# A hybrid decoder step: the output projection by seven half-size products a pair, and the residual added later and by columns

## The chip, the cores and the metric

The kernel runs on one core of one Trainium2 chip. The core has a matrix engine (TensorE, PE in the profile), a vector engine (VectorE, DVE), a scalar engine (ScalarE, ACT), GpSimd (POOL) and a sync engine (SP) that only issues transfers; transfers run on 16 DMA engines. ACT, DVE and PE each take their instructions in program order and wait at the head of their queue; POOL computes a little and issues its own transfers, among them all that add to what lies at their destination. The metric is the device time of one execution in microseconds (us), the median of several.

## The reference, and what is computed

One step of a decoder layer for 1024 prompt tokens and 8 x 8 sample tokens, T = 1088 token columns, width 1024, all in fp32:

```
xn = RMSNorm(x)
q, k, v, a, b, gate_a, gate_b = split(xn @ w_in)
A = windowed attention(q, k, v) @ w_o ;  B = silu(LayerNorm(conv31(a * sigmoid(b)))) @ w_pb
h = x + (sigmoid(gate_a) * A + sigmoid(gate_b) * B) @ w_out        # the output projection
up = RMSNorm(h) @ w_up                                             # 1024 -> 2 x 2816
y = RMSNorm(h + (silu(conv3(up)[:2816]) * conv3(up)[2816:]) @ w_down)
```

Call the merged branches (the bracket ahead of w_out) M. What the change touches is M @ w_out, the RMSNorm and the first up-projections that follow, and the place where h, the residual, is added to the result of w_down.

## The kernel before

Activations lie with the features in the 128 partitions and the tokens along the row. A product in fp32 is made as three matmuls of rounded words (`mm3`): every operand x is held as a high word, x rounded, and a low word, x minus the high word; the matmuls are high by high, high by low and low by high. Making the words is a *split* (`split_ps`, for weights `w_parts`): ACT casts, DVE subtracts.

The stages, with their place in the profiled execution (us): the input projection with attention and convolution in between, ending in the two gates (to some 648); w_o (to 748); w_pb, with M formed and split as it comes out (`do_pb`, to 843); the output projection (843 to 942); three plain up-projections f = 0, 1, 2 (to 1015); nineteen further ones as *pairs* (1015 to 1464); the down-projection in three *rounds* (to 1626), and a tail that does the last four features plainly and applies the last norm (to the end).

A *pair* is a Strassen-Winograd product: a 2 x 2 product of halves takes seven half-size products in place of eight, at the price of sums of weights (s1 to s4), sums of activations (T1 to T4) and additions of results. In the up stage the sums of activations are made once (`sums`, all four quarters of the tokens), the sums of weights on DVE for each pair (`plan_pair`, line 1172). In the down stage the sums of weights are made ahead in DRAM by POOL's transfers (`folds`, line 617, tensor d_wd), six dependent stages a pair, two transfers in the first two stages and one in the others.

The output projection is plain: eight blocks m of 128 output features, each over four quarters of 272 tokens and eight blocks of inputs, 8 x 4 x 8 x 3 = 768 matmuls of 272 columns. Evacuation (`ev_out`) adds x from DRAM, squares on ACT and sums the squares on DVE for the norm. The last four m run quarter by quarter, and after each quarter `norm2` makes the norm, splits the normed quarter, and has POOL store h to DRAM (d_h, line 1006). `sums` follows in f = 0; it forms each normed value again from its two words (line 1131). A plain up-projection ends in `finish`, a convolution on ACT and DVE (line 1082), gate, and a store of the product (d_x) from which the down stage reads its operands (x, line 1304); in a pair, `finish` of the feature is placed in the queues 100 steps later (UP_LATER).

In the last round, (r, j) = (2, 0) in the code, POOL adds h from d_h onto the results held in H by sixteen accumulating transfers of 272 KB, four after each of the products n = 0, 1, 3 and 4 (line 1421). The tail then walks through the columns in three chunks of 352, 352 and 256 (TAIL_CHUNKS).

The order on each engine is made by a scheduler from the priorities of the program; `later` moves a piece back, and `in_order` ties a piece to the instructions written just ahead of it. The functions are these:

## Time and profile before

| | us |
|---|---|
| median of three runs (lowest, highest) | 1683.46 (1680.57, 1689.4) |
| the profiled execution | 1688.82 |
| its span | 1686.9 |
| PE busy in it | 1658.0 (98%) |
| DVE busy | 1320.3 (78%) |
| ACT busy | 885.2 (52%) |
| POOL busy | 299.9 (18%) |

The span is the time from the first to the last instruction in the trace; 1.9 us of the profiled execution lie outside it. "Busy" is the time in which an engine had at least one instruction in work, and waits are put down to the engine or transfer that ended them. The row of PE's clock gives the share of full speed that was granted. A matmul's row lasts longer than the distance to the next one, since matmuls are pipelined.

### The profile page before, as it was taken

How to read it: one execution, taken by the hardware profiler on the slowest of the kernel's cores; microseconds unless marked ns; L12 is line 12 of the kernel's file. 1: busy time of each engine (PE TensorE's matmuls, PEld its weight loads, DVE VectorE, ACT ScalarE, POOL GpSimd, SP SyncE). 2: the span in 40 equal slices, each digit the busy share in tenths (PEclk: the TensorE clock that was granted, in tenths of full speed). 3: DMA queues.
4: the chain of work that ended last, by engine and by line, in shares of the span. 5: the costliest groups of instructions: out<-in, count | busy, mean ns of one | idle time of the engine just before them, and what ended most of it. 6: DMA issues, size and time to landing. Idle time of an engine off the chain costs nothing. (4 is left out here: it accounts for less than half of the span.)

```text
span 1686.9 us, 30229 instructions
## 1 busy us (share of the span) xinstructions
PE 1658.0 (98%) x11656; PEld 1639.0 (97%) x11656; DVE 1320.3 (78%) x2400; ACT 885.2 (52%) x1807; POOL 299.9 (18%) x541
## 2 busy tenths in 40 slices
PE   9999999999999999999999998999999999999998
PEld 8999999999999999999999997999999999998998
DVE  7899999999669995865546896778778777976556
ACT  7434477743588745973333454444444446833222
POOL 0210112130011111110000154333333210001100
PEclk9999999999999999999999999999999999999999
DMA  6122213242211255544343336676766544758713
GB/s 210 42 51 70 63 58 115 61 143 58 82 45 47 81 211 170 174 161 135 126 141 105 89 126 166 179 180 173 180 173 173 142 109 174 259 181 234 173 65 106
DMA packets 114015, 220.56 MB, mean 131 GB/s; under 512 B 24384, under 2 KB 63440, under 8 KB 113568
## 3 DMA queue, kind: packets, MB, share of 16 engines
q1 hardware_dynamic: 85328, 136.99, 26.5%
q0 software_dynamic: 27968, 81.12, 18.2%
q8 instruction: 91, 1.49, 0.4%
q10 hardware_dynamic: 576, 0.53, 0.1%
q14 instruction: 52, 0.43, 0.1%
HBM read 158.21 MB, written 81.24 MB: 142 GB/s over the span
## 5 line engine op out<-in xcount | busy, mean ns | idle before, releaser
L198 PE MATMUL mm<-xh,whi 128*128 128x384 f32 (+1 forms) x920 | 306.9, 334 | 0.8 <-ACT whi L179 0.8
L199 PE MATMUL mm<-xl,whi 128*128 128x384 f32 (+1 forms) x920 | 301.2, 327 | 0.0
L200 PE MATMUL mm<-xh,wlo 128*128 128x384 f32 (+1 forms) x920 | 300.9, 327 | 0.0
L198 PEld LDWEIGHTS mm<-xh,whi 128*128 128x128 f32 x920 | 173.5, 189 | 2.2 <-ACT whi L179 1.4
L199 PEld LDWEIGHTS mm<-xl,whi 128*128 128x128 f32 x920 | 173.6, 189 | 1.1 <-DVE xl L262 0.2
L200 PEld LDWEIGHTS mm<-xh,wlo 128*128 128x128 f32 x920 | 173.2, 188 | 0.1
L1082 DVE SCALAR_TENSOR_TENSOR acc<-st,fc,acc 128x1104 f32<-128x1104 f32 x88 | 119.7, 1364 | 3.2 <-ACT acc L1080 1.4
L198 PE MATMUL mm<-mh,whi 128*128 128x272 f32 x368 | 106.7, 290 | 1.0 <-ACT st L1073 1.0
L199 PE MATMUL mm<-ml,whi 128*128 128x272 f32 x368 | 106.1, 288 | 0.0
L200 PE MATMUL mm<-mh,wlo 128*128 128x272 f32 x360 | 104.1, 289 | 0.0
L179 ACT CAST whi<-wraw 128x1024 fp32r<-128x1024 f32 (+1 forms) x71 | 69.1, 977 | 64.2 <-PE mm L199 49.1
L180 DVE TENSOR_TENSOR wlo<-wraw,whi 128x1024 fp32r<-128x1024 f32 (+1 forms) x71 | 80.0, 1130 | 16.8 <-ACT whi L179 16.6
L477 DVE SCALAR_TENSOR_TENSOR bt<-u,consts,bt 128x513 f32<-128x513 f32 x120 | 89.6, 747 | 0.6
L477 DVE SCALAR_TENSOR_TENSOR c<-sm,hsum,c 128x512 f32<-128x512 f32 x120 | 89.4, 745 | 0.6
L477 DVE SCALAR_TENSOR_TENSOR c<-u,consts,c 128x512 f32<-128x512 f32 x112 | 83.4, 744 | 0.2
L198 PE MATMUL mm<-th,whi 128*128 128x272 f32 x240 | 70.0, 292 | 4.5 <-DVE st L1204 3.6
L198 PEld LDWEIGHTS mm<-mh,whi 128*128 128x128 f32 x368 | 69.2, 188 | 1.3 <-ACT st L1073 1.3
L199 PE MATMUL mm<-tl,whi 128*128 128x272 f32 x240 | 70.1, 292 | 0.0
L200 PE MATMUL mm<-th,whi 128*128 128x272 f32 x240 | 69.9, 291 | 0.0
L199 PEld LDWEIGHTS mm<-ml,whi 128*128 128x128 f32 x368 | 69.4, 188 | 0.0
L330 ACT ACTIVATE p<-p,nm 128x257 f32<-128x257 f32 (+1 forms) x128 | 62.2, 489 | 12.0 <-DVE nm L325 11.7
L200 PEld LDWEIGHTS mm<-mh,wlo 128*128 128x128 f32 x360 | 67.7, 188 | 0.0
(609 smaller groups left out, 5640.5 us busy)
## 6 DMA issues: line engine op xcount, KB each, us to landing
wraw<-wall SPq DMA_DIRECT2D x113, 512.0 KB, 3.8
d_x<-st POOLq DMA_DIRECT2D x27, 544.0 KB, 6.2
d_wd<-wall POOLq DMA_DIRECT2D x54, 256.0 KB, 5.9
x<-d_x SPq DMA_DIRECT2D x14, 544.0 KB, 5.6
d_x<-acc POOLq DMA_DIRECT2D x9, 816.0 KB, 8.0
wraw<-wall SPq DMA_DIRECT2D x27, 256.0 KB, 4.0
x<-d_x SPq DMA_DIRECT2D x14, 408.0 KB, 3.8
d_wd<-d_wd POOLq DMA_DIRECT2D x18, 256.0 KB, 4.5
```

What stands on the lines that cost most here:

```text
L179: self.nc.scalar.copy(h[:, z], r[:, z])
L180: self.nc.vector.tensor_tensor(l[:, z], r[:, z], h[:, z].bitcast(F32), ALU.subtract)
L198: mm(ps, wh, xh, start=first, stop=False, skip_group_check=more)
L199: mm(ps, wh, xl, start=False, stop=False, skip_group_check=more)
L200: mm(ps, wl, xh, start=False, stop=last, skip_group_check=more)
L330: nc.scalar.activation(pt[:, j, lo:width + 1], pt[:, j, lo:width + 1], AF.Exp, bias=nm[:, j:j + 1], scale=-1.0, accum_out=den[:, j:j + 1])
L477: mac = lambda o, x, w: nc.vector.scalar_tensor_tensor(o, x, w, o, ALU.mult, ALU.add)
L1082: nc.vector.scalar_tensor_tensor(acc, st[:, k:k + AW], fw(f, k), acc, ALU.mult, ALU.add)
```

## The change

**The output projection** takes the blocks m two by two, four pairs of seven half-size products, each over two quarters and four blocks of inputs: 4 x 7 x 2 x 12 = 672 matmuls. The sums of the weights are made in DRAM (d_wo) by POOL, eight transfers of 256 KB a pair in six stages (`fold_stages`), one stage put ahead of each stream of the input phase from the twelfth weight on. T1 is formed and split in `do_pb`, whose blocks now run in the order 0, 4, 1, 5, 2, 6, 3, 7; T2 to T4 are formed there and split in the first pair. The last pair runs by quarters. Results are added up in H, now eight tiles (a quarter by half the features).

**norm2** works in place in H and comes in the order of quarters 2, 0, 3, 1; h is stored by POOL ahead of it. **f = 0 and f = 1** run side by side, quarter by quarter (`plain_side`), norm2 of the next quarter in between; `sums` takes the normed values from H, in two calls, without forming them from words. `finish` of f = 0, 1, 2 is not moved back. Several buffers lie elsewhere.

**The residual** is added by columns: columns 0 to 271, four rows after product 4 and four after product 5 of the last half round (2, 1); columns 272 to 703 after the rounds; columns 704 to 1087 in the first chunk of the tail. Ahead of each group POOL copies one column of the last result ("mark"). The tail's chunks are 272, 432 and 256. `in_order` now covers POOL too.

```diff
-TAIL_CHUNKS = [(0, 352), (352, 352), (704, 256)]
+TAIL_CHUNKS = [(0, 272), (272, 432), (704, 256)]
...
+FOLD_FROM = 12
+PB_ORDER = (0, 4, 1, 5, 2, 6, 3, 7)
+LATE_QUARTERS = (2, 0, 3, 1)
...
+    def fold_stages(self, a, b, c, d, to):
+        s = [to[k] for k in range(4)]
+        return [[(s[0], c), (s[3], a)], [(s[0], d, ALU.add), (s[3], c, ALU.add)], [(s[1], s[0])],
+                [(s[1], a, ALU.add)], [(s[2], s[1])], [(s[2], b, ALU.add)]]
...
+            if FOLD_FROM <= n:
+                with self.in_order():
+                    self.fold(next(out_folds, ()))
...
+                if y == 0 and c == 2:
+                    live["12"], live["t1"] = right, left
+                    add(left, right, left)
+                    for j, (h, l) in enumerate(B[T1]):
+                        self.split_ps(h[:, kk, :], l[:, kk, :], left[:, j * QW:(j + 1) * QW])
+                if y and c == 1:
+                    add(word[T2][:, kk, :], right, live["t1"])
+                    add(word[T3][:, kk, :], live["12"], right)
+                if y and c == 0:
+                    add(word[T4][:, kk, :], left, word[T2][:, kk, :])
...
+        seq = (("A", "11", 0, 0, True), ("E", T1, 1, 1, True), ("A", T2, 0, 1, False), ("E", "22", 0, 1, False),
+               ("A", T3, 1, 1, False), ("C", "21", 0, 0, True), ("A", T4, 1, 0, False))
...
+        def product(p, n, j):
+            bank, b, u, half, fresh = seq[n]
+            m, c = 2 * p + u, 2 * half + j
...
+            hs = H[c, m // 4][:, m % 4, :]
...
+            for k in range(KT // 2):
+                ks = slice(k * P, (k + 1) * P)
+                self.mm3(ps, wh[:, ks], wl[:, ks], xh[:, k, :], xl[:, k, :], fresh and k == 0, k == KT // 2 - 1, not fresh)
...
+            add(hs, t if first else hs, ps, ALU.subtract if u == 0 and bank != "C" else ALU.add)
+            if last:
+                nc.scalar.activation(t if m else ssq[c], hs, AF.Square)
+                if m:
+                    add(ssq[c], ssq[c], t, ALU.add)
...
+                for x in (k, k + 1):
+                    hs = H[c, y][:, x % 4, :]
+                    nc.vector.scalar_tensor_tensor(hs, hs, self.c("g2", x), ssq[c], ALU.mult, ALU.mult)
+                self.split_ps(hh[c][y][:, ks, :], hl[c][y][:, ks, :], H[c, y][:, ks, :])
...
+            for n, c in enumerate(LATE_QUARTERS):
+                norm = norm2(LATE_QUARTERS[n + 1]) if n < 3 else iter(())
+                next(norm, None)
+                if n == 0:
+                    ws += [self.weight(("up", x), 0) for x in fs[2:]]
+                if n == 2:
+                    sums(0)
+                for x in (0, 1, 2, 3) if n < 3 else (2, 3, 0, 1):
+                    self.stream(None, xs, both[x][3], chunks=(c,), w=ws[x], table=QUARTERS)
+                    for _ in norm:
+                        pass
+            sums(1)
+            for f in range(2):
+                finish(f, both[2 * f:2 * f + 2])
...
-                        add(r, hh[c][y][:, ks].bitcast(F32), hl[c][y][:, ks].bitcast(F32))
...
-            if (r, j) == (2, 0):
-                for top, half in {0: ((0, 0),), 1: ((4, 0),), 3: ((0, 1),), 4: ((4, 1),)}.get(n, ()):
-                    cs = slice(half * HT, (half + 1) * HT)
-                    for row in range(top, top + 4):
-                        nc.gpsimd.dma_start(H[row][:, cs], self.d_h[row, :, cs], accum_op=ALU.add)
+            if (r, j) == (2, 1) and n in (4, 5):
+                residual(hs, range(4 * n - 16, 4 * n - 12), slice(*TAIL_CHUNKS[0]))
...
+        residual(hs, range(KT), slice(o1, o1 + w1))
...
+                if c == 0 and m == 4:
+                    residual(hs, range(KT), slice(o1 + w1, T))
```

What this does to the order on the engines, at three places. First **POOL in the input phase**. In the names, p and sp are the tiles of the softmax, into which POOL copies the sink; kp is a load of old keys, d_c and o_cb* are stores, u gets zeros. A bracket names what an instruction waits for; DMASW and DMAHW are landings of transfers. Before:

```order
L319 COPY p_2946<-nsink_83 128x4 [waits PE_49,Activation_49,Pool_49]
L500 DMA d_c_59<-u_1494 128x1024 [waits DMASW4_49,DVE_49]
L672 DMA o_cbp<-u_2383 128x30 [waits DMASW5_49,DVE_49]
L673 DMA o_cbs<-u_2383 1024x1x30 [waits DMAHW5_49,DMASW6_49,DVE_49]
L643 MEMSET u_3032 128x30 [waits DMASW4_49,DMASW3_49]
L644 MEMSET u_3032 128x2
L319 COPY p_2996<-nsink_83 128x4 [waits PE_49,Activation_49,Pool_49]
L411 DMA kp_3322<-kpT 128x256 [waits DMASW7_49,DMASW0_49,PE_49]
```

and now, in the same place:

```order
L320 COPY p_2957<-nsink_84 128x4 [waits PE_49,Activation_49,Pool_49]
L501 DMA d_c_59<-u_1495 128x1024 [waits DMASW6_49,DVE_49]
L611 DMA d_wo_65<-wall 128x512 [waits DMASW7_49,DMASW4_49]
L611 DMA d_wo_65<-wall 128x512 [waits DMASW5_49,DMASW0_49]
L686 DMA o_cbp<-u_2391 128x30 [waits DMASW1_49,DVE_49]
L687 DMA o_cbs<-u_2391 1024x1x30 [waits DMAHW5_49,DMASW2_49,DVE_49]
L611 DMA d_wo_65<-d_wo_65 16x4096 [waits DMASW7_49,DMASW3_49]
L320 COPY p_3007<-nsink_84 128x4 [waits PE_49,Activation_49,Pool_49]
L657 MEMSET u_3045 128x30 [waits DMASW6_49]
L658 MEMSET u_3045 128x2
L412 DMA kp_3336<-kpT 128x256 [waits PE_49]
L611 DMA d_wo_65<-wall 128x512 [waits DMASW3_49]
```

Between the two copies into p three transfers of the sums have come in (two more stand just ahead of the first copy): the second stage, two 128x512 that each wait for a landing of the first, and the third, the 16x4096 one, which waits for a landing of the second. The fourth follows the load of kp and waits for the third.

Second **DVE in f = 0**: the sums for the pairs. Before, each first forms four values from the words mh and ml:

```order
L1131 TENSOR_TENSOR s_10326<-mh_1203_9533,ml_1205_9535 128x544
L1131 TENSOR_TENSOR s_10328<-mh_1245_9855,ml_1247_9857 128x544
L1131 TENSOR_TENSOR s_10330<-mh_1246_9856,ml_1248_9858 128x544
L1131 TENSOR_TENSOR s_10332<-mh_1204_9534,ml_1206_9536 128x544
L1131 TENSOR_TENSOR s_10326<-s_10328,s_10326 128x544 [waits DVE_49]
L1131 TENSOR_TENSOR s_10328<-s_10330,s_10328 128x544 [waits DVE_49]
L228 TENSOR_TENSOR tl_1288_10075<-s_10326,th_1280_10067 128x544 [waits Activation_49]
L1131 TENSOR_TENSOR s_10330<-s_10330,s_10326 128x544 [waits DVE_49]
L228 TENSOR_TENSOR tl_1292_10079<-s_10328,th_1284_10071 128x544 [waits Activation_49]
L1131 TENSOR_TENSOR s_10332<-s_10332,s_10330 128x544 [waits DVE_49]
L228 TENSOR_TENSOR tl_1290_10077<-s_10330,th_1282_10069 128x544 [waits Activation_49]
L1131 TENSOR_TENSOR s_10346<-mh_1203_9533,ml_1205_9535 128x544
```

and now, with th the tiles of H:

```order
L1268 TENSOR_TENSOR th_1136_8921<-th_1140_8925,th_1136_8921 128x544
L229 TENSOR_TENSOR ml_1327_10415<-th_1137_8922,mh_1325_10413 128x544 [waits Activation_49]
L1268 TENSOR_TENSOR th_1140_8925<-th_1141_8926,th_1140_8925 128x544 [waits DVE_49]
L1268 TENSOR_TENSOR th_1136_8921<-th_1140_8925,th_1136_8921 128x544
L1268 TENSOR_TENSOR th_1141_8926<-th_1141_8926,th_1136_8921 128x544 [waits DVE_49]
L1268 TENSOR_TENSOR th_1140_8925<-th_1141_8926,th_1140_8925 128x544 [waits DVE_49]
L1268 TENSOR_TENSOR th_1137_8922<-th_1137_8922,th_1141_8926 128x544 [waits DVE_49]
```

The additions of mh and ml are gone; the four subtractions of each step remain, and the splits follow them.

Third **POOL at the end of the down stage**, the transfers that add h onto the results, whose tiles now bear the names mh to tl. Before, in the first half of the last round, the first eight of sixteen:

```order
L1421 DMA th_1833_15851<-d_h_63 128x544 [waits DMASW2_49,DVE_49]
L1421 DMA th_1835_15860<-d_h_63 128x544 [waits DVE_49]
L1421 DMA tl_1837_15871<-d_h_63 128x544 [waits DVE_49]
L1421 DMA tl_1839_15880<-d_h_63 128x544 [waits DVE_49]
L1421 DMA mh_1822_15802<-d_h_63 128x544 [waits DMAHW6_49,DMASW6_49,DVE_49]
L1421 DMA mh_1824_15811<-d_h_63 128x544 [waits DVE_49]
L1421 DMA ml_1826_15828<-d_h_63 128x544 [waits DMASW0_49,DVE_49]
L1421 DMA ml_1828_15837<-d_h_63 128x544 [waits DMASW1_49,DVE_49]
```

and now, in the second half of it:

```order
L1514 COPY mark_17849<-tl_1804_15880 128x1 [waits DVE_49,Activation_49]
L1517 DMA mh_1787_15802<-d_h_63 128x272 [waits DMASW6_49,PE_49]
L1517 DMA mh_1789_15811<-d_h_63 128x272 [waits PE_49]
L1517 DMA ml_1791_15828<-d_h_63 128x272
L1517 DMA ml_1793_15837<-d_h_63 128x272
L1514 COPY mark_17917<-ml_1793_15837 128x1 [waits DVE_49]
L1517 DMA th_1798_15851<-d_h_63 128x272 [waits DMASW2_49,PE_49]
L1517 DMA th_1800_15860<-d_h_63 128x272 [waits PE_49]
L1517 DMA tl_1802_15871<-d_h_63 128x272 [waits DMASW4_49]
L1517 DMA tl_1804_15880<-d_h_63 128x272 [waits DMASW5_49]
L1514 COPY mark_17975<-tl_1804_15880 128x1 [waits DVE_49,Pool_49]
```

The first eight have half the columns they had, stand in the second half of the round, behind a mark, and two more groups of eight (432 and 384 columns) follow the third mark and a fourth.

More of the change, by code (lines that the diff above doesn't have):

```diff
@@ L1008, in phase_z @@
[L1008 to L1016 removed]
+        z_es.close()
+        l_es, h_es, wt_es = ExitStack(), ExitStack(), ExitStack()
@@ new lines, in phase_z @@
+        pairs = KT // 2
+        for p in range(1, pairs - 1):
+            for n in range(7):
+                i = 7 * p + n
+                w_load2(15 if i < 12 else i + 4 if i < 18 else 28)
+                w_split2(i + 3)
+                for j in range(2):
+                    product(p, n, j)
+        w_split2(28)
+        norm = norm2(2)
+        for j in range(2):
+            for n in range(7):
+                product(pairs - 1, n, j)
+                if n in (4, 6):
+                    store(6 - n + j)
+                if j == 0 and n == 0:
+                    while len(self.w_raw) < n_up + 2:
+                        self.w_load()
+                if j == 0 and n == 4:
+                    with self.in_order():
+                        while len(self.w_hl) < n_up + 2:
+                            self.w_split()
+                if j and n % 2 == 0:
+                    with self.in_order():
+                        next(norm)
+            if not j:
+                next(norm)
@@ L1227, in ffn @@
             plan_pair(f)
-        for f in range(PLAIN):
+        plain_side()
+        for f in range(2, PLAIN):
             plain(f)
-            if f == 0:
-                with self.later(SUM_LATER):
-                    sums()
         steps = [(r, j, n) for r in range(len(ROUNDS)) for j in range(2) for n in range(7)]
@@ L1257, in ffn @@
         free += [(0, f"w{z}{x}") for z in ("hi", "lo") for x in range(2)]
-        free += [(12, f"d{x}") for x in range(3)]
+        free += [(4 * (x < 2), f"th{x}1") for x in range(4)]
         free.sort(key=lambda x: x[0])
@@ L1373, in ffn, with residual @@
         ops = (ALU.add, ALU.subtract, ALU.add, ALU.add, ALU.subtract, ALU.subtract, ALU.subtract)
+        def residual(after, rows, cs):
+            mark = nc.gpsimd.tensor_copy(self.t(dt, [P, 1], "mark", bufs=2), after[:, 0:1])
+            with tc.issue_after(mark.ins):
+                for row in rows:
+                    nc.gpsimd.dma_start(H[row][:, cs], self.d_h[row, :, cs], accum_op=ALU.add)
         for s, (r, j, n) in enumerate(steps):
```

289 lines of the change are left out of this document (170 added, 119 removed).

## The prediction

> **What bounds the kernel now.** First the page: is one engine the limit?
>
> ```profile
> span 1686.9 us, 30229 instructions
> PE 1658.0 (98%) x11656; PEld 1639.0 (97%) x11656; DVE 1320.3 (78%) x2400; ACT 885.2 (52%) x1807; POOL 299.9 (18%) x541
> DVE  7899999999669995865546896778778777976556
> ```
>
> PE is busy for 98% of the span, so two things shorten it: fewer matmuls, and fewer gaps. Next, busy time by stage (columns: length, then busy us and instructions of PE, weight load, DVE, ACT, POOL; the granted clock; DMA share; GB/s).
>
> ```profile
> 843.00:943.00 100.00, 99.88 (x783) 99.01 (x782) 59.35 (x122) 34.03 (x69) 2.70 (x3) 1.00 0.42 125
> 1015.00:1047.00 32.00, 24.25 (x174) 22.97 (x173) 19.86 (x31) 11.88 (x24) 14.01 (x24) 0.95 0.72 195
> 1464.00:1533.00 69.00, 68.69 (x549) 68.47 (x548) 56.90 (x108) 32.16 (x50) 0.00 (x0) 1.00 0.66 204
> 1533.00:1582.00 49.00, 43.97 (x328) 42.69 (x327) 21.57 (x39) 11.60 (x11) 13.95 (x16) 0.97 0.89 207
> ```
>
> The output projection (first row) has no gap: 99.88 us for 783 matmuls, 0.1276 us each. Two stages do: the first pair, idle for 32 - 24.25 = 7.75 us, and the first half of the last round, idle for 49 - 43.97 = 5.03. These idle times are low by some 0.16 us a gap, because a matmul's row lasts 290 ns, not 128 (row in the third part): with five and six gaps, 8.6 and 6.0 us. Who ends the gaps, in each of the two (waiting line, releaser: us, times, longest):
>
> ```profile
> PE mm L198 <- DVE st L1204: 3.6, 1, 3.6
> PE aux L198 <- ACT st L1222: 1.5, 1, 1.5
> PE mm L198 <- ACT st L1073: 1.0, 1, 1.0
> ...
> PE mm L198 <- ACT x L1311: 1.7, 1, 1.7
> PE mm L199 <- DVE x L228: 0.9, 1, 0.9
> ```
>
> In the pair it is ACT's and DVE's evacuation (st); in the round the splits of x, and behind these the chain of waits shows transfers (start, us, what):
>
> ```profile
> 1025.75 0.51 POOL d_x L1110
> 1035.23 8.06 DMA wraw<-wall
> ...
> 1539.95 15.78 DMA x<-d_x
> 1555.83 1.11 ACT x L227
> 1556.97 1.30 DVE x L228
> 1564.50 10.95 DMA x<-d_x
> ```
>
> So the loads of x take 15.78 and 10.95 us. Over the program they take 5.6, and in that window software transfers (POOL's) hold half of the moved time, because POOL adds h there:
>
> ```profile
> x<-d_x SPq DMA_DIRECT2D x14, 544.0 KB, 5.6
> ...
> q0 software_dynamic: 2129, 4.14, 50.3%
> th<-d_h POOLq DMA_DIRECT2D x4, 272.0 KB, 8.5
> ```
>
> A gap may also cost clock. Two stretches after a gap:
>
> ```profile
> 1044.40:1047.80 3.40, 3.33 (x16) 3.33 (x17) 3.17 (x4) 0.21 (x1) 2.58 (x6) 0.56 0.31 127
> 1549.10:1552.50 3.40, 3.40 (x15) 3.40 (x16) 1.27 (x4) 1.04 (x1) 0.86 (x1) 0.51 1.07 271
> ```
>
> After the 3.6 us wait the clock was 0.56 for 3.4 us, and at 1549, behind waits of 1.7 and 0.9, it was 0.51. So the two stages lose another 1.5 and 1.7 us: 10.1 us in the first pair and 7.7 in the round.
>
> The Trainium skill, "TensorE: Matmul & The Clock Gate", section "Why this matters for your kernels", asks for no idle gaps of more than about 3 us to keep the clock. By that, the round's gaps would cost no clock; the row at 1549 shows that two shorter ones did, so here I follow the row. By the page the round's term would be 6.0 instead of 7.7.
>
> **The change part by part.** The durations that I use (line, engine, tiles, shapes, count | busy, mean ns):
>
> ```profile
> L198 PE MATMUL mm<-mh,whi 128*128 128x272 f32 x128 | 37.1, 290 | 0.0
> ...
> L984 DVE TENSOR_TENSOR H<-mm,xr 128x272 f32<-128x272 f32 x32 | 13.6, 434 | 24.5 <-PE mm L200 24.4
> L989 DVE TENSOR_TENSOR ssq<-ssq,xr 128x272 f32<-128x272 f32 x26 | 11.4, 437 | 7.9 <-ACT xr L988 7.6
> L1003 DVE SCALAR_TENSOR_TENSOR nt<-H,consts,ssq 128x272 f32<-128x272 f32 x24 | 10.6, 493 | 0.0
> L180 DVE TENSOR_TENSOR wlo<-wraw,whi 128x1024 fp32r<-128x1024 f32 x5 | 6.1, 1223 | 1.3 <-ACT whi L179 1.3
> ...
> L1131 DVE TENSOR_TENSOR s<-mh,ml 128x544 f32<-128x544 f32 x16 | 10.7, 716 | 0.0
> L1082 DVE SCALAR_TENSOR_TENSOR acc<-st,fc,acc 128x1104 f32<-128x1104 f32 x16 | 21.4, 1359 | 0.6 <-ACT acc L1080 0.6
> L228 DVE TENSOR_TENSOR wlo<-s,wlo 128x512 fp32r<-128x512 f32 x5 | 3.4, 688 | 1.1 <-ACT wlo L227 1.1
> ```
>
> *Matmuls.* 96 of 768 go, on the path and with nothing beside them: 96 x 0.1276 = **-12.2 us**.
>
> *DVE in the projection.* It now has 7 x 2 additions a pair, 56 x 0.434 = 24.3; 28 sums of squares, 12.2; 28 weight splits of 512, 28 x 0.688 = 19.3; six splits of T2 to T4 of 1088 columns, 6 x 1.30 (x in the chain, as wide) = 7.8; four up weights, 4.9; the first norm2, 8 x 0.493 and 4 x 0.716, 6.8. That is 75 us in 672 x 0.126 = 85 us, 89% where it was 59%. The page's DVE row shows 90% and more over nine slices on end, so 89% can be kept up, but the work must come in time. In the quarter-by-quarter stage of f = 0 and 1, 384 matmuls or 48 us, DVE has three norm2 of 6.8 and a pair of weight splits (2 x 1.22), the subtractions (16 x 0.716) and their splits (16 x 0.716): 46 us, 95%. Beside PE this is free; where it lags, PE waits. I count the places where the next matmul needs the newest work: second and last pair (about 1 us each), start of the up stage (1), start of f = 2, whose weights are split behind all sums (2). **+5 us**, between 0 and 12: the latter if DVE got through 121 us of work at 85% of its time, 121/0.85 - 133 = 9, and a clock spell of 1.7 came on top.
>
> The sixteen additions of T1 to T4 in the w_pb stage, 16 x 0.716 = 11.5 us, fall where DVE is free for half the time (window row: 48.63 busy of 96):
>
> ```profile
> 747.00:843.00 96.00, 96.00 (x586) 96.00 (x585) 48.63 (x102) 32.35 (x64) 0.54 (x1) 1.00 0.45 147
> ```
>
> With 60 of 96 that stays hidden, zero.
>
> *First pair.* Its gaps come of a backlog: the sums of f = 0 with 16 additions of words that now vanish (10.7 us), and the finish of f = 1, whose store (d_x at 1025.75) came 10 us after the pair began. Now 192 matmuls of f = 2, 24 us, lie between the end of f = 1 and the pair; the two finishes take DVE some 17 us (eight rows of 1.36 and the gates' products), so that the store comes some 7 us ahead of the pair. That is 17 us earlier, and the longest wait is 3.6, so nearly all should go; the load of raw weights that took 8.06 us remains, at a DMA share of 0.72. I take **-8.8** of 10.1, between -4 (the 3.6 us gap and its clock stay) and -10.1.
>
> *Last round.* The sixteen additions of h leave it. With 5.6 us for a load the one issued at 1539.95 lands at 1545.6 and is split by 1548, ten us ahead of 1558.3, the end of the DVE row; the one of 1564.5 by 1572.5, five ahead of when it came. The gap of 1.7 hangs on the load before these, which I take to be slow in the same way. **-7.4** of 7.7; at worst -4, since the share was 0.66 already in the stage before, without h.
>
> *The residual later.* One issue of the kind on POOL, and the tail's stage:
>
> ```profile
> 1563.78 0.87 POOL L1421 DMA_DIRECT2D ml<-d_h  x1 [0.18 <-issue]
> ...
> 1626.00:1687.00 61.00, 54.55 (x371) 52.59 (x369) 34.49 (x77) 16.44 (x37) 0.00 (x0) 0.99 0.21 74
> ```
>
> Columns 0 to 271 are issued in the last three products and needed from the first tail rows on; those of 432 columns behind them take 8 x 0.87 us to issue and 8.5 to land, done some 15 us into the tail; its first chunk of 8 x 12 matmuls lasts 12 us, and its second begins with row 0, which is issued first. **+0.5**, between 0 and 3.
>
> *POOL in the input phase.* 32 transfers in 24 stages; each stage waits for the one before, with copies for the softmax behind it. A stage takes 4.5 to 5.9 us by the same kind of transfers in the up stage:
>
> ```profile
> d_wd<-wall POOLq DMA_DIRECT2D x54, 256.0 KB, 5.9
> ...
> d_wd<-d_wd POOLq DMA_DIRECT2D x18, 256.0 KB, 4.5
> ...
> 260.67 0.19 POOL L319 COPY p<-nsink 128x4 f32<-128x4 f32 x1 [0.26 <-PE aux L363]
> ...
> 276.83 0.51 ACT L330 ACTIVATE p<-p,nm 128x257 f32<-128x257 f32 x1
> PE aux L363 <- ACT p L334: 1.5, 1, 1.5
> ```
>
> Where the first stages stand (near 257 us), two landings come ahead of the copy of 260.67: it slips by some 4 us, to 265. ACT uses that tile at 276.83, so 12 us are left. **+1**, between 0 and 6 (two gaps like the last row's, with a clock spell each).
>
> For the same stage the Trainium skill, "DMA: Bandwidth & Descriptors", section "Anatomy of one DMA", gives about 2 us and the bytes at 436 GB/s; by an estimate from that page a 256 KB stage takes 2.6 us and the copy would slip by about 1, so the term would be 0. The rows with 4.5 and 5.9 are of a busier stage; I keep them.
>
> *Sum* on the profiled execution, 1686.9 + 1.9 = 1688.8: -12.2 + 5 - 8.8 - 7.4 + 0.5 + 1 = -21.9, to 1666.9. It is 5.4 above the median of the runs, 1683.46, so against that: 1661.6, **1662 us**.
>
> **The rivals.**
>
> *DVE becomes the bound* of projection and first up stage. For it: 89 and 95%, and the rows in which it waits for ACT in between. Against it: nine slices at 90%. Price: the +12 instead of +5, with 2 more lost in the first pair: 1671.
>
> *The residual's traffic is only moved*: it delays the tail. For it: 8.5 us a transfer and the issue in a row on POOL. Against: a DMA share of 0.21 in the tail. Price: second and third chunk late by 3 us each with one spell, +7: 1669.
>
> *The gaps stay*, since they are not what I take them for: the change doesn't relieve what it moves. The pair's last wait hangs on the raw weights, and the loads of x may be slow by their own volume. Then -12.2, -4, -0 and +6.5 remain: 1674 to 1678, say 1676.
>
> *POOL holds up the attention*: slower. Place: the stages near 257, 340 and 460 us; the mechanism is a softmax copy behind landings. It decides once a copy slips beyond the 12 us left, that is, when the two landings ahead of it take six us more each, 10 to 12 us, twice what I take. Each of the dozen softmax groups behind a stage would then cost a gap of 1.5 and a spell of 1.7, 38 us in all: 1700. Against it: POOL idle for 82% of the span.
>
> **How the numbers follow.** Forecast 0.60; DVE the bound 0.17; residual late 0.08; gaps stay 0.09; POOL 0.06. The forecast's own range is 1654 to 1670. The best sum (-12.2 - 10.1 - 7.7) gives 1653.5, and the runs of one kernel spread by 4 either way, hence the low end at 1649; the upper end takes in DVE, residual and most of the third rival: 1679. A measurement of this kernel can tell about 0.5%, 8.4 us, from no change, that is 1675. Faster 0.82 (forecast, most of the next two), same 0.12 (the third, with scraps of the others), slower 0.06.
>
> **What would show it.** In the new profile: 672 matmuls of 272 columns in 85 to 89 us, DVE near 0.9 there; no wait over 1 us in the first pair, and a clock of 1.00; loads of x below 7 us in the last round with no wait for their splits; copies into p later by a few us, with the waits of the input phase as before. I am wrong if PE waits for DVE over 8 us between 843 and 1015, if the tail waits for d_h, or if new waits for p stand before 650 us.

## The result, and the profile after

The changed kernel takes **1673.99 us** in the median of six runs (1672.58 to 1678.05); the kernel before, on the same chip, takes 1685.39 (1680.57 to 1689.4, six runs). The ratio is **0.9934, with a 95% interval of 0.9913 to 0.9956**: 11 us faster, where 21.9 by the profiled execution were forecast. The change is real, and half of what was expected is missing. The profiled execution took 1672.8 us, 16.0 less than that of before. All times here are of runs at the usual clock; one run of an experiment, 2297.63 us at a granted clock of 0.654 (the residual alone, in the kernel before), is left out.

The page first; then the busy time in the four stages that the prediction names (length, then busy us and instructions of PE, weight load, DVE, ACT, POOL; granted clock; DMA share; GB/s), in the order projection, f = 0 and 1, first pair, first half of the last round.

```profile
span 1671.0 us, 30330 instructions
PE 1644.2 (98%) x11616; PEld 1626.5 (97%) x11616; DVE 1338.9 (80%) x2430; ACT 893.7 (53%) x1817; POOL 315.7 (19%) x589
```

```profile
841.80:931.90 90.10, 87.62 (x698) 86.75 (x697) 63.74 (x130) 39.14 (x73) 5.29 (x7) 1.00 0.59 182
931.90:984.10 52.20, 52.20 (x428) 52.20 (x427) 46.90 (x83) 30.85 (x61) 11.46 (x17) 1.00 0.25 51
1008.20:1040.10 31.90, 23.45 (x170) 22.79 (x170) 17.87 (x28) 11.33 (x21) 7.43 (x14) 0.89 0.61 163
1526.60:1568.60 42.00, 42.00 (x339) 42.00 (x338) 24.37 (x41) 12.45 (x13) 0.00 (x0) 1.00 0.48 147
```

The last half round has become what it should be: no gap, clock 1.00. The first pair has not: PE is busy for 23.45 us of 31.90, as before, and the clock is lower still. Where the time went can be set out stage by stage, each from the start of its first matmul to that of the next stage's first:

| stage, us | before | after | difference | forecast |
|---|---|---|---|---|
| up to the projection | 843.4 | 841.8 | -1.6 | +1 |
| projection | 99.1 | 90.1 | -9.0 | |
| f = 0 and 1 | 48.9 | 52.2 | +3.3 | |
| these two together | 148.0 | 142.3 | -5.7 | -12.2 + 5 = -7.2 |
| first pair | 31.7 | 31.9 | +0.2 | -8.8 |
| last round, first half | 50.3 | 42.0 | -8.2 | -7.4 |
| tail, its three chunks | 46.0 | 45.9 | -0.1 | +0.5 |

All other stages agree within 0.3 us. So one term is wholly missing, the first pair, and the rest came close. In medians less is left than in these two executions: the one of before lies 3.4 us above its median of six, the one of the change 1.2 below its own.

**The first pair.** Who ends PE's gaps there (waiting line, releaser: us, times, longest):

```profile
PE mm L199 <- ACT st L1360: 6.2, 1, 6.2
PE aux L201 <- DVE wlo L229: 1.5, 1, 1.5
PE aux L199 <- ACT wlo L228: 0.8, 1, 0.8
```

The longest wait has grown from 3.6 to 6.2 us. It is for an evacuation (st, line 1360), a copy of 0.4 us. What ACT does up to then (start, us, operation, and in brackets how long ACT sat idle before it and for whom):

```profile
996.78 0.44 ACT L1198 COPY st<-mm 128x208 f32<-128x208 f32 x2
...
1011.55 0.62 ACT L228 CAST whi<-th 128x512 fp32r<-128x512 f32 x1 [2.62 <-issue]
1014.59 0.62 ACT L228 CAST wlo<-wraw 128x512 fp32r<-128x512 f32 x1 [2.41 <-PE aux L201]
1020.38 0.62 ACT L228 CAST wlo<-th 128x512 fp32r<-128x512 f32 x1 [5.18 <-PE aux L201]
1020.90 1.30 ACT L1205 ACTIVATE acc<-st,fc 128x1104 f32<-128x1104 f32 x1
1025.05 1.12 ACT L1213 ACTIVATE acc<-acc 128x1104 f32<-128x1104 f32 x1 [2.84 <-DVE acc L1207]
1026.08 0.66 ACT L1360 COPY st<-mm 128x272 f32<-128x272 f32 x2
```

The first row is the last copy of f = 2's gate. After it ACT is not busy, it waits. At 1015.2 it has nothing at hand but a weight split (line 228) that belongs to the second pair. That split writes into a buffer which PE is still reading, and so it stands at the head of ACT's queue for 5.18 us, until PE has finished that product. Behind it stand the convolution of f = 2's gate (line 1205), whose input was complete at 997.2, its activation (1213), and only then the evacuation that PE needs. PE, once it has released the split, needs the bank that this evacuation has to read first, and waits for all that stands between. The late convolution also keeps its input buffer. POOL, which clears a buffer for the next result, waits for it:

```profile
1025.16 0.10 POOL L1182 MEMSET st<- 128x2 f32 x1 [15.90 <-DVE acc L1207]
```

By the order of the clearings this is the buffer of the pair's second result; that of the first, into which the copy at 1026.08 goes, was cleared at 1005.4. So the 6.2 us wait is the queue's, but copies into the second result could not have come much sooner either.

The chain of waits shows DVE in the same position (start, us, what):

```profile
1008.78 6.20 DMA th<-wall
...
1015.61 1.28 DVE th L1310 x2
1016.90 0.61 DVE wlo L229
1017.55 0.39 PE aux L201
...
1022.24 1.38 DVE acc L1207
1023.65 1.38 DVE acc L1207
...
1026.08 0.38 ACT st L1360
1026.50 0.59 PE mm L199
```

The sums of weights for the second pair (line 1310), which wait for a load of 6.20 us, stand ahead of a split for the *first* (wlo, 1016.90), for which PE waits 1.5 us; and two steps of the gate's convolution (line 1207) lie right ahead of the evacuation.

The backlog that I had held responsible is gone, and the gaps are there. POOL's rows show when f = 1 was finished:

```profile
1000.35 0.74 POOL L1235 DMA_DIRECT2D d_x<-st  x1 [5.35 <-DVE st L1226]
```

Its first store is issued at 1000.35, 8 us ahead of the pair. The prediction had "some 7".

**Projection, f = 0 and 1.** PE's waits between 842 and 981, all of them:

```profile
PE aux L199 <- DVE th L951: 1.0, 1, 1.0
PE mm L200 <- DVE t3l L229: 0.8, 1, 0.8
PE mm L199 <- DVE th L951: 0.7, 1, 0.7
```

That is 2.5 us of waiting for DVE, less than my +5. But 384 matmuls of f = 0 and 1 take 52.2 us without a gap, and at the pitch of f = 2 (24.21 us for 192) they should take 48.4. The groups of the same stretch (line, engine, shapes, count | busy, mean ns | idle before) show what else PE does:

```profile
L295 PE MATMUL aux<-consts,rows 68*128 68x68 f32 x32 | 4.0, 268 | 0.0
L291 PE MATMUL aux<-mean,ssq 128*68 128x1 f32 x32 | 2.4, 196 | 0.0
```

and in the same stretch of the kernel before, in their place:

```profile
L997 PE MATMUL aux<-ssq,mean 128*128 128x272 f32 x8 | 2.8, 427 | 0.1
```

The norm after the projection is made by 64 rows of small matmuls instead of eight of wide ones (32 products in the code instead of four; each shows as two rows). By the distances between starts, the small ones take 5.1 us of PE's time and the wide ones took 1.3. They come from `rstd_steps` in the new norm2, and I had no term for them.

**The last half round.** The loads of x in it, from issue to landing; after, and then before (the same view, each for its own half round):

```profile
x<-d_x SPq DMA_DIRECT2D x8, 544.0 KB, 3.9
```

```profile
x<-d_x SPq DMA_DIRECT2D x7, 544.0 KB, 11.0
```

A median of 3.9 us instead of 11.0, and PE waits for nothing from there to the end of the program. The tail, which now gets its residual late, is as long as before.

### The profile page after: what moved, and what is told of

The parts are those of the page before. It is cut to its first block, busy times and chain, and to the rows that moved or that the text cites. A ratio compares the mean times of both kernels' runs of the same rounds, so it can differ in the third digit from the quotient of the medians.

```text
span 1671.0 us, 30330 instructions
## 1 busy us (share of the span) xinstructions
PE 1644.2 (98%) x11616; PEld 1626.5 (97%) x11616; DVE 1338.9 (80%) x2430; ACT 893.7 (53%) x1817; POOL 315.7 (19%) x589
## 5 line engine op out<-in xcount | busy, mean ns | idle before, releaser
L180 ACT CAST whi<-wraw 128x1024 fp32r<-128x1024 f32 (+1 forms) x65 | 62.7, 971 | 59.0 <-PE mm L200 49.9
L181 DVE TENSOR_TENSOR wlo<-wraw,whi 128x1024 fp32r<-128x1024 f32 (+1 forms) x65 | 72.6, 1122 | 15.1 <-ACT whi L180 14.8
L228 ACT CAST wlo<-th 128x512 fp32r<-128x512 f32 x56 | 35.1, 627 | 66.6 <-PE aux L201 42.9
L1360 ACT COPY st<-mm 128x272 f32<-128x272 f32 (+2 forms) x133 | 44.3, 350 | 49.1 <-PE mm L201 49.1
L1342 DVE TENSOR_TENSOR st<-st,aux 128x272 f32<-128x272 f32 (+2 forms) x95 | 34.2, 379 | 39.2 <-PE aux L201 37.7
L201 PE MATMUL mm<-sh,wlo 128*128 128x384 f32 (+1 forms) x192 | 62.6, 326 | 0.0
L200 PE MATMUL mm<-sl,whi 128*128 128x384 f32 (+1 forms) x192 | 62.6, 326 | 0.0
L199 PE MATMUL mm<-sh,whi 128*128 128x384 f32 (+1 forms) x192 | 62.6, 326 | 0.0
```

What stands on the lines that cost most here:

```text
L180: self.nc.scalar.copy(h[:, z], r[:, z])
L181: self.nc.vector.tensor_tensor(l[:, z], r[:, z], h[:, z].bitcast(F32), ALU.subtract)
L199: mm(ps, wh, xh, start=first, stop=False, skip_group_check=more)
L200: mm(ps, wh, xl, start=False, stop=False, skip_group_check=more)
L201: mm(ps, wl, xh, start=False, stop=last, skip_group_check=more)
L228: self.nc.scalar.copy(h, src)
```

## The experiments

After the result my theory of the first pair was this: **the order of the queues** makes the gaps. Work that waits for PE or for a load has been placed ahead of work that PE waits for, and an engine that takes its instructions in order then idles with PE. Its rivals were a **backlog** of DVE and ACT (the prediction's reading), and the **late load** of raw weights by itself. The other runs measure the terms of the norm, the residual and POOL apart. Ratios are to the kernel before, run beside each experiment.

### First pair: splits tied behind the evacuations

In a pair's steps, the weight splits of the first pair from the seventh on, and the first two of the second, are kept in program order:

```diff
-                prep(base + n + 1 + AHEAD)
+                with ExitStack() as es:
+                    if f == PLAIN and n > 2 or f == PLAIN + 1 and n < 2:
+                        es.enter_context(self.in_order())
+                    prep(base + n + 1 + AHEAD)
```

> The changed kernel, with the weight splits of the first pair from the seventh on, and the first two steps of the second pair, kept in program order behind the evacuations. Theory (order): the first pair's gaps come of what stands in the queues ahead, not of the amount of work. DVE's 1.7 us gap behind the second pair's sums goes, and the 6.3 us gap falls to some 2, since ACT no longer waits for a slot of the second pair; the first pair takes about 26 us where it took 31.9, and the time is 5 to 6 us below the changed kernel, 1668. Rival (backlog): ACT and DVE have too much to do there; the gaps move but their sum stays, 31 to 32 us, 1674. Rival (late raw weights): the load of the second pair's weights lands 6 us after f = 2 ends whatever the order; the gap moves into the second pair and the two together stay at 53 us, 1674.

Measured: 1666.11 us, ratio 0.9884 (0.987 to 0.9899). The first pair falls from 31.9 to 24.6 us. PE's longest wait in it:

```profile
PE mm L199 <- ACT st L1363: 1.9, 1, 1.9
```

The convolution on ACT now starts at 1014.89 instead of 1020.90, and the 6.2 us wait is a 1.9 us one. No instruction was taken out, so most of the gap was order.

### First pair: the convolution ahead as well

Beside the ties, now from the sixth split on, the convolution of f = 2's gate is kept ahead of the fifth split:

```diff
+            if f == PLAIN - 1:
+                self.conv = first, last
...
+                    if f == PLAIN and n == 1:
+                        for x in self.conv:
+                            es.enter_context(tc.issue_after(x.ins))
+                    if f == PLAIN and n > 1 or f == PLAIN + 1 and n < 2:
+                        es.enter_context(self.in_order())
```

Here first and last are the convolution's first instruction (ACT) and its last (DVE).

> As the one before, and also the convolution of f = 2's gate is kept ahead of the fifth weight split on ACT and DVE, and the sixth split behind the first evacuations. Theory (order): with the buffer of f = 2's gate free some 20 us earlier, the first evacuation stands behind nothing that waits; no gap over 1 us and no slow clock in the first pair, 21.2 to 23 us for it, 10 us below the changed kernel: 1664. Rival (backlog): 30 us or more for the pair, the time within 3 us of the changed kernel's 1674. Rival (late raw weights): a gap of 2 to 6 us shows up in the second pair in place of it.

Measured: 1661.96 us, ratio 0.9863 (0.9848 to 0.9877). The pair's stage:

```profile
1007.20:1029.10 21.90, 21.45 (x171) 21.23 (x170) 15.77 (x25) 10.81 (x21) 8.04 (x14) 1.00 0.89 241
```

21.9 us, clock 1.00, where an undisturbed pair takes 21.2. The DMA share is even higher than in the changed kernel (0.89 for 0.61), so the transfers of this stage are not what slows it.

### First pair: the convolution alone

To separate the two parts, only the convolution is kept ahead, of the splits from the fifth on; nothing is tied behind the evacuations:

```diff
-                prep(base + n + 1 + AHEAD)
+                with ExitStack() as es:
+                    if f == PLAIN and n > 0:
+                        for x in self.conv:
+                            es.enter_context(tc.issue_after(x.ins))
+                    prep(base + n + 1 + AHEAD)
```

> The changed kernel with one order only: the gate convolution of the third pass (f=2) is kept ahead of the first pair's weight splits from the fifth on; nothing is tied behind the first pair's evacuations. Theory (the queues' order makes the first pair's gaps, and two things stand in front: the convolution behind the splits, and the second pair's splits and sums ahead of the first pair's evacuation): the convolution is done before the pair, so the 6.3 us gap shrinks, but the evacuation still stands behind the second pair's first split, and the second pair's sums still stand ahead of the first pair's last split on DVE: first pair 23 to 27 us against 31.9 in the changed kernel, 24.6 with the ties alone and 21.9 with both; ratio to before 0.987 to 0.991. Rival (the convolution alone was the cause, the ties of the earlier runs did nothing): the pair falls to 21.9, ratio 0.986. Rival (the late raw load of the second pair alone is the cause): the pair stays at 30 to 32, ratio 0.993.

Measured: 1663.77 us, ratio 0.9886 (0.9869 to 0.9903); the pair takes 22.8 us, just below what I had expected of my theory, and close to the rival "the convolution alone". ACT's rows tell why:

```profile
1009.35 1.32 ACT L1205 ACTIVATE acc<-st,fc 128x1104 f32<-128x1104 f32 x1
...
1017.18 0.66 ACT L1366 COPY st<-mm 128x272 f32<-128x272 f32 x2
...
1023.97 0.62 ACT L228 CAST wlo<-th 128x512 fp32r<-128x512 f32 x1 [2.06 <-PE aux L201]
```

The scheduler has re-sorted the queue by itself: the second pair's split, which stood ahead of the evacuation at 1020.38, now stands behind it, at 1023.97. So I had been wrong that the two obstacles are independent. With the convolution ahead, 9.1 of the 10.7 us go; with the ties alone, 7.3; with both, 10.0. (These are single profiled executions; that one is ahead of the next by less than 2 us isn't settled by them.)

### The same order in the kernel before

The decisive test for the backlog: the kernel *before*, with its 16 additions of words and its late finish of f = 1, and only the order of the second experiment.

```diff
+                    if f == PLAIN and n == 1:
+                        for x in self.conv:
+                            es.enter_context(tc.issue_after(x.ins))
+                    if f == PLAIN and n > 1 or f == PLAIN + 1 and n < 2:
+                        es.enter_context(self.in_order())
```

> The kernel before with the queue order of e2_conv_first in its first pair: the convolution of f = 2's gate ahead of the fifth weight split, later splits behind the evacuations. Theory (order): there too the gaps come of what stands ahead in the queues; the first pair goes from 31.7 to 22 to 25 us and the time to 1676. Rival (backlog, as the prediction had it for this kernel): DVE still has the sixteen additions and f = 1's finish to do when the pair begins; the pair takes 28 us or more, the gaps only move, and the time is 1682 to 1685.

Measured: 1675.34 us, ratio 0.9944 (0.9926 to 0.9962). First pair and last half round:

```profile
1013.40:1034.60 21.20, 21.20 (x171) 21.20 (x170) 15.83 (x25) 10.81 (x21) 5.81 (x14) 1.00 0.80 243
1520.80:1568.40 47.60, 44.09 (x337) 43.66 (x337) 21.96 (x39) 10.66 (x11) 13.47 (x16) 0.96 0.92 216
```

No gap at all in the pair: 21.2 us instead of 31.7, with the whole of the alleged backlog in place. It falls. ACT's rows of the kernel before show the same fault that the changed kernel has:

```profile
1018.85 0.62 ACT L227 CAST wlo<-wraw 128x512 fp32r<-128x512 f32 x1 [11.16 <-PE aux L200]
1023.12 0.62 ACT L227 CAST wlo<-s 128x512 fp32r<-128x512 f32 x1 [3.65 <-PE aux L200]
1023.64 1.30 ACT L1073 COPY st<-mm 128x272 f32<-128x272 f32 x5
```

ACT idles for 11.16 us ahead of a split that waits for PE, and again for 3.65; the five copies behind it are f = 2's, whose matmuls ended at 1015.6. A few lines of order in the kernel before are worth 9 us, nearly as much as the whole change.

### The residual in its old place

The changed kernel, with h added by sixteen transfers of 272 KB in the first half of the last round, as before; the chunks of the tail stay as changed.

```diff
-            if (r, j) == (2, 1) and n in (4, 5):
-                residual(hs, range(4 * n - 16, 4 * n - 12), slice(*TAIL_CHUNKS[0]))
+            if (r, j) == (2, 0):
+                for top, half in {0: ((0, 0),), 1: ((4, 0),), 3: ((0, 1),), 4: ((4, 1),)}.get(n, ()):
+                    cs = slice(half * HT, (half + 1) * HT)
+                    for row in range(top, top + 4):
+                        nc.gpsimd.dma_start(H[row][:, cs], self.d_h[row, :, cs], accum_op=ALU.add)
...
-        residual(hs, range(KT), slice(o1, o1 + w1))
...
-                if c == 0 and m == 4:
-                    residual(hs, range(KT), slice(o1 + w1, T))
```

> The changed kernel with h added again by sixteen transfers of 272 KB in the first half of the last round; the tail's chunks stay 272, 432 and 256. Theory (contention with x): the loads of x take 10 us and more again, the half round takes 50 us where it took 42.0, with a spell of slow clock, and the time is 8 us above the changed kernel: 1682. Rival (the loads of x are slow by their own volume, and what made the round shorter is something else of the change): it stays at 42 to 43 us, 1674. The tail should take the same 46 us in both.

Measured: 1682.18 us (eight runs), ratio 0.9981 (0.9968 to 0.9994). The half round takes 54.3 us instead of 42.0:

```profile
1524.20:1578.50 54.30, 46.52 (x338) 45.24 (x337) 25.11 (x43) 12.52 (x13) 13.90 (x16) 0.94 0.84 196
```

```profile
x<-d_x SPq DMA_DIRECT2D x8, 544.0 KB, 8.6
```

The loads of x take 8.6 us, where the change has 3.9 and the kernel before 11.0 (I had expected 10 and more), and PE waits for their splits. The tail does not get shorter by it.

### The residual alone, in the kernel before

```diff
-TAIL_CHUNKS = [(0, 352), (352, 352), (704, 256)]
+TAIL_CHUNKS = [(0, 272), (272, 432), (704, 256)]
...
+            if (r, j) == (2, 1) and n in (4, 5):
+                residual(hs, range(4 * n - 16, 4 * n - 12), slice(*TAIL_CHUNKS[0]))
```

with the two later groups as in the change, and the sixteen additions taken out.

> The kernel before with only the residual by columns and the tail's chunks of 272, 432 and 256. Theory (contention with x): the first half of the last round takes 42 us in place of 50.3, the tail as long as before (46 us for its three chunks), and the time is 8 us below the kernel before: 1677. Rival (the loads of x are slow by their own volume): 50 us, no change. Its input stage is that of the kernel before, unchanged, and shows how far 843.4 us, the end of that stage, moves from run to run: 843 if the 1.6 us that the changed kernel gained there are real, 841 to 842 if they are scatter.

Measured: 1677.0 us (four runs), ratio 0.9954 (0.9937 to 0.9971), that is 7 to 8 us of the change's 11. The half round takes 42.1 us with no gap:

```profile
1531.00:1573.10 42.10, 42.10 (x339) 42.10 (x338) 23.52 (x41) 11.62 (x11) 0.00 (x0) 1.00 0.45 140
```

So this part works alone and is the larger one. The first pair, whose program is that of before, takes 29.4 us in this execution instead of 31.7: its last wait is 2.4 us instead of 3.6, and no slow clock follows. So the stage differs by that much between executions of one program.

### The norm by one wide product

The changed kernel, with the norm's factor made as before, by one 272-wide product a quarter and a reciprocal of 128 x 272 on DVE:

```diff
-            yield from self.rstd_steps(lp, ssq[c], ssq[c], QW)
+            ps = self.bank("aux")
+            nc.tensor.matmul(ps[:, :QW], self.mean, ssq[c], start=True, stop=True)
+            self.rstd(ssq[c], ps[:, :QW])
+            yield
```

> The changed kernel with the norm's factor made as in the kernel before: one product of 272 columns with the means and a reciprocal of 128x272 on DVE, in place of sixteen small matmuls and a reciprocal of 68x4 a quarter. Theory (uncounted matmuls): the 64 small matmul rows of the four quarters cost PE 5.1 us against 1.3, so projection and f = 0, 1 take 138.5 us in place of 142.3 and the time falls by 3 to 4 us, 1670. Rival (DVE is the bound there): four reciprocals of 1.85 us make DVE later by 7 us in a stage in which it is 90% busy; 142 us or more, 1674 to 1680.

Measured: 1668.44 us, ratio 0.9899 (0.9883 to 0.9916). From the start of the projection to the end of f = 2 it takes 163.8 us instead of 166.5. So the wide form gives back 2.7 us. By the distances between starts the norm's own matmuls take 4.0 us less here, and 1.4 are lost again between other matmuls. The pair was 30.7 us here and the input phase 1.3 us shorter, so not all of the lower median belongs to the norm.

### Order and norm together

The second experiment's order and the wide product in one kernel.

> The changed kernel with the queue order of e2_conv_first and the wide norm of e4_wide_norm together. If the two gains are independent: 2.7 us less than e2_conv_first in projection and f = 0 to 2, the first pair at 22 us, 1659. Rival (the reciprocals make DVE late for the sums and f = 2, and the first pair, now without slack, pays it back): 1662 or more, with gaps behind DVE between 930 and 1030 us.

Measured: 1661.34 us (1657.86 to 1662.95), ratio 0.9857 (0.9841 to 0.9873). It beats both kernels; from the second experiment, at 1661.96, it cannot be told apart, though its projection and f = 0 to 2 are 2.2 us shorter. Its input phase came out 1.8 us longer in the profiled execution. With the pair's order mended, the change comes to the time that had been forecast. That it does so to a microsecond is in part luck, since single terms were off by up to 2.6 us.

### POOL's sums of weights later in the input phase

```diff
-FOLD_FROM = 12
+FOLD_FROM = 20
```

One stage is put ahead of each stream from the twentieth weight on, instead of the twelfth, so the first softmax copies have none in front.

> The changed kernel with the stages of the weight sums from the twentieth weight on in place of the twelfth, so that other copies for the softmax stand behind them. Theory (POOL's waits are covered): the input stage ends at 840 to 842 us as in the changed kernel, the list of PE's waits before 650 us is the same within 0.5 us, 1674. Rival (the sums hold up the attention): waits for p or pth come or go, and the end of the input stage moves by over 1.5 us.

Measured: 1674.31 us, ratio 0.9937 (0.9922 to 0.9951), the same as the changed kernel. The projection starts at 842.8 us. PE's waits for the softmax up to 650 us, in the changed kernel:

```profile
PE aux L376 <- ACT pth L228: 1.4, 2, 1.0
PE aux L364 <- ACT p L335: 1.3, 1, 1.3
```

and with the later sums:

```profile
PE aux L376 <- ACT pth L228: 2.7, 2, 1.7
PE aux L364 <- ACT p L335: 1.4, 1, 1.4
```

They are no shorter; the first is 1.3 us longer, beyond the 0.5 that I had allowed, but not in the direction of the rival. POOL's part in the input phase costs nothing that can be measured here: over all kernels above, changed or not, the projection starts between 840.1 and 843.6 us.

The first pair, the same program as in the changed kernel, took 35.1 us in this execution instead of 31.9. Its waits are 0.8, 1.9 and 6.2 us instead of 0.8, 1.5 and 6.2, and the slow clock begins sooner and lasts for 17 us:

```profile
1017.60:1034.60 17.00, 9.92 (x42) 9.60 (x43) 8.42 (x10) 5.73 (x10) 5.19 (x8) 0.50 0.35 72
```

So where the order is not mended the pair takes 30.7 to 35.1 us in the changed kernel and its variants, and where it is mended 21.9 to 24.6.

## Why the prediction was right or wrong

**The time** lies in the range (1649 to 1679), 12 us above the forecast of 1662. Faster by more than 0.5%, to which I had given 0.82, is what the ratio shows, though its interval reaches down to 0.44%.

**Matmuls, -12.2, and DVE's lag, +5: right, with one item left out.** Together -7.2 were forecast and -5.7 measured. The waits for DVE come to 2.5 us by the trace; the rest of the excess, some 4 us, is nearly all the norm's small matmuls, for which I had no term: by their rows they take 3.8 more than the wide ones of before, and the wide form gave back 2.7. My count of DVE's work was too high in the projection (75 us, 89%; the window has 63.74 of 90.10, 71%); in f = 0 and 1 it was right (46 us; the window has 46.90 of 52.20). The row of the page that I quoted for it has eight slices at 90% on end, not nine. The rival "DVE becomes the bound" is refuted: PE waits 2.5 us for it, not 8.

**First pair, -8.8: wrong, and this is the step that failed.** "Its gaps come of a backlog" was the sentence. Every part of the mechanism that I named took place: the additions of words vanished, and f = 1's product was stored 8 us ahead of the pair. The gaps remained, because they hang on neither. With the backlog restored and the order mended (the kernel before with the order) the pair takes 21.2 us; with the backlog gone and the order left, 31.9. The size of the term, 10.1 to be had, was right: the order takes it from 31.9 to 21.9. The late load of raw weights that I left standing was not the limit either, since at 0.89 of DMA share the pair runs almost without a gap; it costs time only because it waits in DVE's queue ahead of what PE needs.

I could have seen it. The row that I quoted for the pair had DVE busy for 19.86 us of 32 and ACT for 11.88. An engine that is late from a backlog is busy all the time; these idled. I had asked who releases PE, and not what the releaser had been doing in the microseconds before.

**Last half round, -7.4: right.** It measured -8.2, the loads of x fell to 3.9 us (I had put them at 5.6), and both runs that move the residual alone, one into the old kernel and one out of the new, show it: 50.3 to 42.1, and 42.0 to 54.3. **The residual later, +0.5: right**, at -0.1: PE waits for nothing in the tail, and the rival that the traffic is only moved falls.

**POOL in the input phase, +1: right in kind.** The copy at 260.67 now starts at 262.34, in a program that ran 1.4 us ahead there, by the copy before it (256.73, now 255.34): a slip of 3.1 where I had 4.

```profile
255.34 0.19 POOL L320 COPY p<-nsink 128x4 f32<-128x4 f32 x1 [0.53 <-PE aux L364]
...
262.34 0.21 POOL L320 COPY p<-nsink 128x4 f32<-128x4 f32 x1
```

It is hidden, as predicted; there are no new waits, and the slower rival, POOL holding up the attention, does not occur. The stages' transfers, which I costed at 4.5 to 5.9 us, are now in the trace:

```profile
d_wo<-wall POOLq DMA_DIRECT2D x24, 256.0 KB, 4.6
...
d_wo<-d_wo POOLq DMA_DIRECT2D x8, 256.0 KB, 3.4
```

The estimate of 2.6 us from the Trainium skill ("DMA: Bandwidth & Descriptors", section "Anatomy of one DMA — SWDGE (gpsimd) path") was too low for both; the rows of the busier stage were the better guide to the first.

**The rival "the gaps stay"** (0.09, at 1676) is what happened in the pair, for a reason other than the one I gave it: not the load, but the order. In the round it was wrong.

**The offset.** I took 5.4 us off because the profiled execution of before stood so far above its median. Over six runs it stood 3.4 above, and that of the change 1.2 below its own. So 16.0 us between the profiled executions are 11.4 between the medians. Profile by profile the terms add up: the pair 9.0 worse than forecast; projection, f = 0 and 1 together 1.5 worse; input phase, round and tail 2.6, 0.8 and 0.6 better; what is left, 0.6, lies in the other stages and in rounding.

**What stays open.** Why the scheduler places f = 2's convolution behind splits of a later product was not settled; only that forcing it ahead re-sorts the rest. Nor is it known why the half round with h in it takes 47.6 in one kernel, 50.3 in another and 54.3 in a third; the medians of the loads of x there, 6.7, 11.0 and 8.6 us, are not in that order. And the experiments on the pair all move the convolution both in ACT's queue and as the holder of its buffer, so what each of the two is worth is not shown.

## What to carry to other kernels

When an engine that is half idle ends PE's wait, read its own queue backwards from the releasing instruction: it may have stood behind something that waited for PE itself. Here taking work off such engines moved nothing, an order did, and a few lines of it were worth as much as a rewritten stage. And when a product is removed, count what the new code adds on the same engine, down to its small matmuls.

## What the runs showed of the hardware

**Gaps close together add up for the clock, within fixed stretches of 3.41 us.** In the kernel before, waits of 1.7 and 0.9 us that ended 1.3 us apart were followed by 3.4 us at a clock of 0.51, and I had taken this against the rule of some 3 us. Other runs have single gaps that are longer and cost nothing. Lost pitch is the distance between the starts of two matmuls beyond the usual 0.126 us. The 3.4 us after a gap of 2.1 us of it (the first experiment, tied splits), and after one of 2.6 (the residual alone, in the kernel before):

```profile
1020.50:1023.90 3.40, 3.40 (x27) 3.40 (x28) 2.31 (x4) 2.42 (x7) 3.40 (x5) 1.00 0.74 117
```

```profile
1043.60:1047.00 3.40, 3.40 (x27) 3.40 (x28) 3.40 (x4) 1.61 (x3) 1.19 (x2) 1.00 0.74 303
```

and after two of 2.7 and 1.2, again 1.3 us apart (the kernel before with the order, last half round), and after the 6.2 us wait of the changed kernel:

```profile
1536.90:1540.30 3.40, 3.40 (x18) 3.40 (x19) 1.31 (x4) 1.05 (x1) 0.86 (x1) 0.62 1.08 295
```

```profile
1026.50:1030.00 3.50, 3.50 (x16) 3.50 (x17) 2.42 (x4) 2.45 (x6) 3.50 (x5) 0.52 0.75 127
```

In lost pitch the pair of gaps in the kernel before comes to 1.9 + 1.2 = 3.1 us. But the sum alone does not decide. In its first pair the changed kernel loses 0.9 and 1.7 us close together, 2.6 in sum, and has the full clock until 1023.0; with POOL's sums later the same two are 0.9 and 2.05, 3.0 in sum, and the clock is down from 1017.6 on, while the second gap still lasts.

What does sort the cases is where the gaps lie. In the record of the granted clock, all changes within one trace lie on a grid of 3.41 us. I added up the lost pitch in each stretch of that grid, in all eleven traces, from 840 us to the last matmul. Of the stretches at full clock, nine hold 2.2 us or more of it, and each of these was followed by half the clock; none that holds 2.0 or less was. The gap of 2.6 us above lies across two stretches and so stays below; the gap of 2.05 shares its stretch with the 0.9 ahead of it. Between 2.0 and 2.2 us no run here has a stretch.

That agrees with the Trainium skill, "TensorE: Matmul & The Clock Gate", section "What's actually happening" (activity is judged over windows of about 3.4 us). The same page of the Trainium skill, section "Why this matters for your kernels", asks for no gap of more than about 3 us; in these traces 2.2 us in one stretch were already enough, so the measurement decides, and the prediction did well to follow its row.
